# Layer 1's values and gates: a product put ahead, and two row block pairs turned by transposing transfers

## The chip, the cores and the metric

The kernel runs on one core of a Trainium2 chip. The metric is the time of one execution in microseconds (us) on the device, as the median of several runs. TensorE (PE) multiplies matrices, VectorE (DVE) and ScalarE (ACT) do elementwise work, GpSimd (POOL) and SyncE (SP) here mostly issue transfers (DMA). Each engine works through its own row of instructions in order, and waits on semaphores for the others.

## What is computed

A trunk of two layers on 1024 rows of 1024 columns in fp32. Each layer is a token mixer and a squared-ReLU MLP, each with an RMSNorm ahead and a residual add behind; layer 0 mixes by dilated attention, layer 1 by gated linear attention (GLA). The change lies at the start of layer 1's mixer, in the part of its first projection that gives the values v and the output gate:

```python
def gla_mixer(h, w_in, w_gate_up, b_gate, norm_w, w_out):
    proj = h @ w_in
    q, k, v = proj[..., :s1], proj[..., s1:s2], proj[..., s2:s3]
    g_out, gate_lr = proj[..., s3:s4], proj[..., s4:]
    gk = gate_lr @ w_gate_up + b_gate
    log_a = jax.nn.log_sigmoid(gk.astype(jnp.float32)) / GLA_GATE_NORMALIZER
    ...
    gate = jax.nn.silu(g_out.astype(jnp.float32)).reshape(B, S, GLA_HEADS, GLA_DV)
    o = (o * gate).reshape(B, S, GLA_VAL_DIM).astype(h.dtype)
    return o @ w_out
```

## The kernel before

**Precision.** Each fp32 operand is cut into a rounded part (hi, by a copy on ACT) and a remainder (lo, by a subtraction on DVE). A product is three matmuls: hi by hi, hi by lo, lo by hi.

**The seven products.** `Mixed` (L901, on `Values`, L766) multiplies the normed rows, transposed, by 1024 columns twice: group g = 0 is the gate (g_out), g = 1 the values. Both are done in Strassen's manner: the rows' transpose has quarters a11, a12, a21, a22, and the seven products of a group use in this order a12, a11, s1, s2, s4, s3, a22 on the rows' side, where s1 = a21 + a22, s2 = s1 - a11, s4 = a12 - s2, s3 = a11 - a21. On the columns' side stand a block of weights or a sum of blocks (`total`, L803), cut into dh (`rounded`, L825, ACT) and dl (`remain`, L833, DVE). Each product has two steps of 24 + 24 matmuls of 128x512; steps 0 to 13 are group 0 and 14 to 27 group 1. `load` (L781) fetches a step's weights, by SP, some steps ahead.

**Accumulators.** The products go in turn to four banks of PSUM called B (pB) and A (pA): "BABABAB", where a new start clears the bank for a12, a11, s1 and a22, and s2, s4 and s3 accumulate on what is there. `sums` (L873) takes results out: c11 is copied from B (a12's product) and added to what A holds after a11, c22, c12 and c21 likewise. For group 0 the results are tiles gq and gp, which then go through the gate's function: `begin` (exp, ACT), `guard` (DVE), `logs` (two ACT operations), `close` (three DVE operations on gd, ge and the result, and a store to ggscr by SP). c21 of a group is added at the start of the next group's first step (L876).

**Buffers.** Tiles come from pools: 25 buffers `k4` of 128 x 1024 fp32 (weights, dh, dl, gp and others), 12 of `h8`, 8 of `t2`.

**Rows and their transposes.** `Halves` (L308) norms the rows and transposes them. The 1024 rows are four row block pairs p of 256 rows. Pairs p = 0 and 1 are turned by transfers: `send` (L332) copies the 32-bit values on ACT into pieces (`half`) in which the two 16-bit halves lie apart, and POOL stores them to a scratch in HBM (`wscr`); `flip` (L341) reads them back with two transposing transfers on SP's queue. Pairs p = 2 and 3, "pairs 3 and 4", are turned on TensorE: `turn` (L347) issues 16 PE transposes of 128x128 (L355) into banks pT, which ACT copies out (L357).

**Order.** All engines' rows are written out by hand, without a scheduler. `Down.run` and `run_end` (L2008, L2122) finish layer 0's MLP; `hook` (L2029) and `between` (L2063) put the norm, the first cuts and the first loads beside its last steps; `gla_values` (L2171) then issues the 28 steps. Behind them stand the low-rank gate's product (L2462, pd), its result lg (L2466, L2467) and the first gate product (L2364, pg).

Of the kernel before, what the change touches and what calls it, by code (L numbers as in the profile page):

```python
# [9 lines left out]
F32 = mybir.dt.float32  # L10
# [3 lines left out]
U16 = mybir.dt.uint16  # L14
AF = mybir.ActivationFunctionType
# [5 lines left out]
P = 128  # L21
D = 1024
# [20 lines left out]
def hybrid_trunk(ctx, tc, x, norm_mix, norm_mlp, norm_fin, a_in, a_out, g_in, g_up, g_b, g_nw,  # L43
                 g_out, m_up, m_down, tab, msk, gmask, ident_d, out):
    nc = tc.nc
    pe, act, dve, pool, sp = nc.tensor, nc.scalar, nc.vector, nc.gpsimd, nc.sync
# [4 lines left out]
    drp = ctx.enter_context(tc.tile_pool(name="drp", bufs=1, space=DRAM))  # L51
# [5 lines left out]
    def k4(shape, dt, name):  # L57
        return wk.tile(shape, dt, name=name, tag="k4", bufs=25)

    def t2(shape, dt, name):  # L60
        return wk.tile(shape, dt, name=name, tag="t2", bufs=8)
# [241 lines left out]
        for j in range(n):  # L303
            yield tuple(s[j][:, :, sl] if len(s) == n else s[0][:, 2 * j:2 * j + 2, sl] for s in sets)

    wscr = [drp.tile([4 * P * D], U16, name=f"wscr{p}") for p in range(2)]

    class Halves:  # L308

# [19 lines left out]
                for k in range(2):  # L329
                    self.a[p // 2, k] = self.one("a", F32)  # L330

        def send(self, p):  # L332

            for i, t in enumerate(self.xn[p]):
                for k in range(2):
                    part = t2([P, D], U16, "half")
                    act.activation(part.rearrange("p (h c) -> p h c", h=2),
                                   t[:, 512 * k:512 * k + 512].bitcast(U16).rearrange("p (c h) -> p h c", h=2), AF.Copy)
                    pool.dma_start(wscr[p].rearrange("(k i p r) -> k i p r", k=2, i=2, p=P)[k, i], part)
# [181 lines left out]
    class Up:  # L521
# [82 lines left out]
        def product(self, p, s, ks=range(4)):  # L604
            w = self.part[p]
            if s == 6:
                wh, wl = w["d"][:, 0], w["d"][:, 1]
            else:
                wh, wl = (t[:, s % 2] for t in w["aabbgg"[s]])
            h = self.h[self.OPERANDS[s]]  # L610
            st = self.st.setdefault(p, {})
            b = "XYXVXZV"[s]
            first = s in (0, 1, 3, 5)
            if first and ks[0] == 0:
                st[b] = bank("p" + b)
            for k in ks:
                xh, xl = h.parts(k)
                for n, (u, v) in enumerate(((wh, xh), (wh, xl), (wl, xh))):
                    pe.matmul(st[b], u[:, k, :], v, start=first and k + n == 0, stop=k == 3 and n == 2,  # L619
                              skip_group_check=True)  # L620
# [145 lines left out]
    class Values:  # L766
# [3 lines left out]
        ahead = (1,)  # L770
# [24 lines left out]
        def source(self, g):  # L795
            return a_in, g * 3 * AW + 2 * AW
# [36 lines left out]
        def remain(self, n):  # L833
# [2 lines left out]
            dve.tensor_tensor(lo, t, hi.bitcast(F32), op=OP.subtract)  # L836
            self.cut[n] = hi, lo

        def product(self, n, blocks=range(4)):
            g, q, m = self.place(n)  # L840
            s = "BABABAB"[q]
            fresh = q in (0, 1, 2, 6)
            if fresh and m == 0 and blocks[0] == 0:
                self.acc[s] = [bank("p" + s) for _ in range(4)]
            th, tl = self.cut[n]
            for k in range(2):
                sh, sl = self.h[ORDER[q]].parts(2 * m + k)
                for t in blocks:
                    c = slice(128 * t, 128 * t + 128)
                    for v, (a, b) in enumerate(((sh, th), (sh, tl), (sl, th))):  # L850
                        pe.matmul(self.acc[s][t], a[:, c], b[:, k, :], start=fresh and m + k + v == 0,  # L851
                                  stop=m == 1 and k == 1 and v == 2, skip_group_check=True)
# [48 lines left out]
    class Mixed(Values):  # L901

        STEPS = 28
        small = True
        ahead = ()

        def __init__(self):
            super().__init__()
# [1 line left out]

        def source(self, g):
            return g_in, (2048, 1024)[g]

        def copy(self, name, s, t, g):
            if g:
# [499 lines left out]
    hs = Halves(x0, wbc, vals, None)  # L1415
# [330 lines left out]
    plan = [n for n in range(8, vals.STEPS) if n // 14 not in vals.ahead or n % 14 > 1]  # L1746
# [52 lines left out]
    for p in range(heads.count):  # L1799
        h, g = divmod(p, NG)  # L1800
        if g == 1 and h:
            plan_merges(h - 1, 14 * p)
        if p == heads.count - 1:
            for k in range(0, KT, 2):
                add_rows(a_out, k)
            c = 14 * p
# [104 lines left out]
    class Down:  # L1911
# [117 lines left out]
        def hook(self, n):  # L2029
            if n == 40:  # L2030
                self.wbc = load_norm_w(self.next_norm)
            if self.spill is not None:
                if n == 46:
                    self.mixed = Mixed()
                    self.hs = Halves(self.xs, self.wbc, self.mixed, self.spill)
                    self.hs.norm(0)
                elif n == 47:
                    self.hs.send(0)
                elif n == 49:
                    self.hs.norm(1)  # L2040
                    self.hs.flip(0)
                elif n == 50:
                    self.hs.send(1)
                elif n >= 52:
                    if n == 52:
                        self.hs.flip(1)
                    for k in range(2):
                        self.mixed.load(2 * (n - 52) + k)
            elif 44 <= n < 48:
                tb = n - 44  # L2050
                o = k4([P, D], F32, "fin")
                y = row_rstd([self.rows(tb)])
                dve.scalar_tensor_tensor(o, self.rows(tb), y[:, 0:1], self.wbc, op0=OP.mult, op1=OP.mult)
                sp.dma_start(out[0, 128 * tb:128 * tb + 128, :], o)
            elif n >= 52:
                for t in (2 * (n - 52), 2 * (n - 52) + 1):
                    ss, o = self.fin[t] = sm([P, 8], "ss"), k4([P, D], F32, "fin")
                    self.square(t, 512, 512, 1)
                    self.weigh(t, 512, 512)
                    dve.tensor_scalar(ss[:, 3:4], ss[:, 1:2], 1.0 / D, EPS, op0=OP.mult, op1=OP.add)  # L2060
                    dve.tensor_scalar(ss[:, 4:5], ss[:, 3:4], -0.5, None, op0=OP.mult)

        def between(self, t):  # L2063

            hs, mixed = self.hs, self.mixed
            if t == 0:
                mixed.rounded(0)
                hs.cut("a12", 0)
                mixed.remain(0)
            elif t == 1:  # L2070
                hs.rstd(2)
                hs.cut("a12", 1)
                mixed.prep(1)
            elif t == 2:
                hs.norm(2)
                hs.cut("a11", 0)
            else:
                hs.rstd(3)
                hs.cut("a11", 1)
                hs.norm(3)  # L2080
                mixed.prep(2)

        def square(self, t, c, n, k):
            ss, _ = self.fin[t]
# [86 lines left out]
    def gla_values():  # L2171

        hs, m = down.hs, down.mixed
        m.product(0)
        hs.turn(2)
        m.prep(3)
        m.load(4)
        m.product(1, [0, 1])
        m.product(1, [2, 3])
        hs.turn(3)  # L2180
        m.load(5)
        hs.sum1(0)
        m.total(4)
        hs.sum1(1)
        hs.cut("s1", 0)
        m.sums(2)
        m.product(2)
        m.rounded(4)
        m.total(5)
        m.remain(4)  # L2190
        hs.cut("s1", 1)
        m.load(6)
        m.sums(3)
        m.product(3)
        m.rounded(5)
        hs.sum2(0)
        m.remain(5)
        hs.sum2(1)
        hs.cut("s2", 0)
        m.load(7)  # L2200
        m.total(6)
        for n in range(4, m.STEPS):
            if n != 13:
                m.guard()
                m.close()
            if n not in (5, 25):
                m.sums(n)
            if n == 4:
                m.sums(5)
                hs.cut("s2", 1)  # L2210
            if n == 24:
                m.sums(25)
            m.prep(n + 2)
            m.load(n + (4 if n < 5 else 5))
            if n == 4:
                m.load(9)
            m.product(n)
            if n == 4:
                hs.sum4()
                hs.cut("s4", 0)  # L2220
            elif n == 5:
                hs.cut("s4", 1)
                hs.sum3()
                hs.cut("s3", 0)
            elif n == 6:
                hs.cut("s3", 1)
                hs.cut("a22", 0)
            elif n == 7:
                hs.cut("a22", 1)
            if n != 13:  # L2230
                m.logs()
                if n >= 7:
                    m.begin()
            if n + 3 < m.STEPS:
                m.total(n + 3)
            if n == 22:
                plan_gla()
                W.limit = 3
            if n == 23:
                W.dma()  # L2240
                W.dma()
            if n in (20, 21):
                hs.cut("a21", n - 20)
            if n >= 25:
                W.pump()
        for t in range(4):
            m.add("c21", "B", t, 1)
        return [[m.h["a11"], m.h["a12"]], [m.h["a21"], m.h["a22"]]]
# [279 lines left out]
```

## Time and profile before

| | |
|---|---|
| Median of 3 runs | 2573.11 us (2571.94 to 2574.34) |
| Profiled execution: its time, its span | 2571.72 us, 2569.9 us |
| Mean granted TensorE clock | 0.999 |
| PE, DVE, ACT busy | 2557.1, 1863.5, 1316.5 us |
| The changed stretch, first product to first pd | 1555.8 to 1712.5 us |

A row of the timeline reads: start and duration in us, engine, line of the kernel, operation, tile written <- tiles read, shape, count; in brackets how long the engine was idle before it and what it waited for. A count over 1 stands for several instructions of a kind in a row, and the duration is then that of all. Matmuls overlap: they last 0.39 us and start every 0.23 us.

### The profile page before, as it was taken

Reading aid. Unit: us, or ns where it says so; the run is one execution under the profiler, and the core shown is the slowest. Engines: PE = TensorE matmul, PEld = TensorE weight load, DVE = VectorE, ACT = ScalarE, POOL = GpSimd, SP = SyncE. Lnnn points to the kernel's source line nnn. Section 1 sums busy time; section 2 is a strip of 40 time slices with the busy share of each in tenths; the row PEclk is TensorE's granted clock in tenths of the full one; section 3 lists DMA queues with packets and bytes.
Section 4 is the critical chain, followed back from the end, with each engine's and each line's share of the span. In section 5 each row is a group of like instructions: output and inputs, shape, how many; then the busy total and the mean of one; then the engine's idle time right before and its main releaser. Section 6 shows DMA issues by size and latency. Waiting matters only on the chain.

```text
span 2569.9 us, 33110 instructions
## 1 busy us (share of the span) xinstructions
PE 2557.1 (100%) x11888; PEld 2131.6 (83%) x11888; DVE 1863.5 (73%) x3018; ACT 1316.5 (51%) x2371; POOL 62.8 (2%) x99
## 2 busy tenths in 40 slices
PE   9999999999999999999999999999999999999998
PEld 7888888888888888888888888888888888888887
DVE  7745888889888778666657588887658866666667
ACT  7423455656666356555533355655436555453344
POOL 0000000000000000000000000000000000000000
PEclk9999999999999999999999999999999999999999
DMA  5543578787887644544865473462724454495543
GB/s 184 172 137 121 144 185 205 187 203 190 200 209 183 227 148 160 164 148 147 292 246 187 139 237 127 134 197 103 201 89 141 164 168 139 145 350 204 188 141 130
DMA packets 403654, 452.10 MB, mean 176 GB/s; under 512 B 93617, under 2 KB 265521, under 8 KB 403490
## 3 DMA queue, kind: packets, MB, share of 16 engines
q1 hardware_dynamic: 397522, 431.84, 55.1%
q0 software_dynamic: 5824, 17.90, 2.0%
q8 instruction: 93, 1.52, 0.3%
q14 instruction: 71, 0.58, 0.1%
q10 hardware_dynamic: 144, 0.26, 0.0%
HBM read 276.04 MB, written 130.81 MB: 158 GB/s over the span
## 4 chain that ended last, share of the span: by engine, by line
PE 64%; DVE 2%; ACT 1%; issue 0%; DMA 0%; SPq 0%; DVEq 0%; ACTq 0%
PE pB L1984 13%; PE pX L619 10%; PE pA L1984 10%; PE pV L619 7%; PE pY L619 3%; PE pZ L619 3%; PE pd L216 3%; PE pd L214 3%; PE pd L215 3%; PE pB L851 3%; PE pA L851 2%; PE pO L2288 1%; PE pU L2270 0%; PE pO L2287 0%; PE pT L355 0%; DVE dl L836 0%
## 5 line engine op out<-in xcount | busy, mean ns | idle before, releaser
L1984 PE MATMUL pB<-dh 128*128 128x512 f32 x512 | 199.2, 389 | 0.0
L1984 PE MATMUL pB<-dl,dh 128*128 128x512 f32 x512 | 199.2, 389 | 0.0
L1984 PE MATMUL pB<-dh,dl 128*128 128x512 f32 x512 | 199.2, 389 | 0.0
L223 DVE TENSOR_TENSOR dl<-sin,dh 128x1024 fp32r<-128x1024 f32 x112 | 136.6, 1220 | 45.5 <-ACT dh L220 44.9
L220 ACT ACTIVATE dh<-sin 128x1024 fp32r<-128x1024 f32 x112 | 117.8, 1052 | 86.9 <-PE pB L1984 35.8
L220 ACT ACTIVATE dh<-kept 128x1024 fp32r<-128x1024 f32 x64 | 67.9, 1061 | 183.5 <-DVE kept L1949 138.1
L619 PE MATMUL pV<-s4h,wd 128*128 128x512 f32 x448 | 150.9, 398 | 0.0
L1984 PE MATMUL pA<-dh 128*128 128x512 f32 x384 | 149.4, 389 | 0.0
L1984 PE MATMUL pA<-dl,dh 128*128 128x512 f32 x384 | 149.4, 389 | 0.0
L1984 PE MATMUL pA<-dh,dl 128*128 128x512 f32 x384 | 149.4, 389 | 0.0
L1026 ACT ACTIVATE pt<-pt,orow 128x128 f32<-128x128 f32 (+1 forms) x192 | 84.5, 442 | 66.2 <-DVE orow L1024 65.6
L1984 PEld LDWEIGHTS pB<-dl,dh 128*128 128x128 f32 x512 | 96.1, 188 | 20.0
L1984 PEld LDWEIGHTS pB<-dh 128*128 128x128 f32 x512 | 96.1, 188 | 20.0
L1984 PEld LDWEIGHTS pB<-dh,dl 128*128 128x128 f32 x512 | 96.1, 188 | 19.9
L557 DVE TENSOR_TENSOR wal<-raw,wah 128x512 fp32r<-128x512 f32 x112 | 76.2, 686 | 38.5 <-ACT wah L556 38.5
L628 ACT ACTIVATE c<-c 128x512 f32<-128x512 f32 x64 | 40.4, 631 | 118.6 <-DVE c L656 77.5
L557 DVE TENSOR_TENSOR wbl<-t,wbh 128x1024 fp32r<-128x1024 f32 x56 | 68.6, 1225 | 44.2 <-ACT wbh L556 44.0
L619 PEld LDWEIGHTS pV<-s4h,wd 128*128 128x128 f32 x448 | 84.2, 188 | 17.8 <-DVE rb L644 0.4
L223 DVE TENSOR_TENSOR dl<-kept,dh 128x1024 fp32r<-128x1024 f32 x64 | 78.4, 1225 | 24.4 <-ACT dh L220 18.4
L619 PE MATMUL pZ<-a22h,wgh 128*128 128x512 f32 x224 | 89.9, 401 | 0.0
L624 ACT ACTIVATE e<-pX 128x512 f32<-128x512 f32 x96 | 56.5, 588 | 63.9 <-PE pX L619 63.8
L619 PE MATMUL pX<-s3h,wgh 128*128 128x512 f32 x224 | 88.6, 395 | 0.0
(404 smaller groups left out, 7409.9 us busy)
## 6 DMA issues: line engine op xcount, KB each, us to landing
sin<-acts SPq DMA_DIRECT2D x112, 512.0 KB, 3.8
raw<-in_mlp_w_up_dram SPq DMA_DIRECT2D x64, 512.0 KB, 6.1
acts<-s SPq DMA_DIRECT2D x64, 512.0 KB, 3.4
raw<-in_mlp_w_down_dram SPq DMA_DIRECT2D x64, 512.0 KB, 4.8
raw<-in_attn_w_in_dram SPq DMA_DIRECT2D x98, 256.0 KB, 4.8
cw<-c SPq DMA_DIRECT2D x192, 128.0 KB, 2.8
acts<-c SPq DMA_DIRECT2D x64, 256.0 KB, 2.2
kept<-in_mlp_w_down_dram SPq DMA_DIRECT2D x32, 512.0 KB, 5.0
```

Source lines behind the costliest of these rows:

```text
L214: pe.matmul(ps, sh, mh, start=start, stop=False)
L215: pe.matmul(ps, sh, ml, start=False, stop=False)
L216: pe.matmul(ps, sl, mh, start=False, stop=stop)
L220: act.activation(hi, src, AF.Copy)
L223: dve.tensor_tensor(lo, src, hi.bitcast(F32), op=OP.subtract)
L557: self.remain(lambda: dve.tensor_tensor(lo, src, hi.bitcast(F32), op=OP.subtract))
L619: pe.matmul(st[b], u[:, k, :], v, start=first and k + n == 0, stop=k == 3 and n == 2, skip_group_check=True)
L624: act.activation(e, self.st[p]["X"], AF.Copy)
L628: act.activation(r, r, AF.Relu)
L851: pe.matmul(self.acc[s][t], a[:, c], b[:, k, :], start=fresh and m + k + v == 0, stop=m == 1 and k == 1 and v == 2, skip_group_check=True)
L1026: act.activation(pt[:, i, :128 * n], pt[:, i, :128 * n], AF.Exp, scale=-1.0, bias=m, accum_out=self.row[:, r, HD:HD + 1])
L1984: pe.matmul(self.acc[s][t], a[:, k, c], b[:, k, :], start=fresh and m + k + v == 0, stop=m == 7 and k == 1 and v == 2, skip_group_check=True)
```

## The change

Group 1's first product (a12, steps 14 and 15) is computed right after group 0's first, by which a list `PLAN` gives the order of the steps: 0, 1, 14, 15, 2 to 13, 16 to 27. It is accumulated in bank A, which is otherwise first used for group 0's a11, and is copied by ACT (`keep`) into two k4 tiles `c11`, which stay until group 1's a11 is there and are then added as before. c11 of group 0 is copied from bank B right after step 1, four copies in a row, rather than in two pairs. c21 of group 0 is added at step 16 rather than 14, and the gate's function of it comes two steps later too; loads, cuts and totals follow the new order. Pairs p = 2 and 3 are turned by `send` and `flip` rather than `turn`: 8 copies on ACT, 8 stores by POOL and 4 transposing transfers on SP's queue, into the scratch `wscr` that now has four parts, in place of 32 PE transposes and 8 copies from PSUM. `send` may now do one half (k) at a time, and the second a11 cut moves from `between` to `gla_values`, behind the sends.

```diff
@@ Halves.send
-        def send(self, p):
-
-            for i, t in enumerate(self.xn[p]):
-                for k in range(2):
+        def send(self, p, ks=(0, 1)):
+
+            for k in ks:
+                for i, t in enumerate(self.xn[p]):
                     part = t2([P, D], U16, "half")
@@ Mixed
-        ahead = ()
+        ahead = (1,)
+        PLAN = (0, 1, 14, 15, *range(2, 14), *range(16, 28))
+        def side(self, g, q):
+            return "A" if q == 0 and g in self.ahead else super().side(g, q)
+
+        def keep(self):
+
+            for t in range(4):
+                if t % 2 == 0:
+                    pair = k4([P, 2, 512], F32, "c11")
+                c = self.kept["c11", t] = pair[:, t % 2, :]
+                act.activation(c, self.acc["A"][t], AF.Copy)
@@ Down.between
                 mixed.prep(1)
+                hs.cut("a11", 0)
             elif t == 2:
                 hs.norm(2)
-                hs.cut("a11", 0)
+                mixed.load(2)
+                mixed.rounded(14)
             else:
+                hs.send(2, (0,))
                 hs.rstd(3)
-                hs.cut("a11", 1)
+                mixed.remain(14)
                 hs.norm(3)
-                mixed.prep(2)
+                mixed.load(3)
@@ gla_values
         m.product(0)
-        hs.turn(2)
+        hs.send(2, (1,))
+        hs.send(3, (0,))
+        m.prep(15)
+        hs.send(3, (1,))
+        m.load(4)
+        hs.flip(2)
+        m.product(1)
+        for t in range(4):
+            m.copy("c11", "B", t, 0)
+        hs.cut("a11", 1)
+        m.prep(2)
+        m.product(14)
+        m.load(5)
+        hs.flip(3)
         m.prep(3)
-        m.load(4)
-        m.product(1, [0, 1])
-        m.product(1, [2, 3])
-        hs.turn(3)
-        m.load(5)
+        m.total(4)
+        m.product(15)
+        m.keep()
+        m.rounded(4)
+        m.remain(4)
+        m.total(5)
         hs.sum1(0)
-        m.total(4)
...
-        for n in range(4, m.STEPS):
+        plan = (*Mixed.PLAN[6:], *range(m.STEPS, m.STEPS + 6))
+        for i, n in enumerate(Mixed.PLAN[6:]):
+            soon = lambda k: plan[i + k]
             if n != 13:
                 m.guard()
                 m.close()
+            if n == 16:
+                for t in range(4):
+                    m.add("c21", "B", t, 0)
+                    m.c["c11", t] = m.kept.pop(("c11", t))
...
-            m.prep(n + 2)
-            m.load(n + (4 if n < 5 else 5))
+            m.prep(soon(2))
+            m.load(soon(4 if n < 5 else 5))
...
-            if n + 3 < m.STEPS:
-                m.total(n + 3)
+            if soon(3) < m.STEPS:
+                m.total(soon(3))
```

More of the change, by code (lines that the diff above doesn't have):

```diff
@@ L304, in pieces @@
             yield tuple(s[j][:, :, sl] if len(s) == n else s[0][:, 2 * j:2 * j + 2, sl] for s in sets)
-    wscr = [drp.tile([4 * P * D], U16, name=f"wscr{p}") for p in range(2)]
+    wscr = [drp.tile([4 * P * D], U16, name=f"wscr{p}") for p in range(4)]
     class Halves:
@@ L837, in remain @@
             self.cut[n] = hi, lo
+        def side(self, g, q):
+            return "BABABAB"[q]
         def product(self, n, blocks=range(4)):
             g, q, m = self.place(n)
-            s = "BABABAB"[q]
+            s = self.side(g, q)
             fresh = q in (0, 1, 2, 6)
@@ L912, in source, with side @@
             return g_in, (2048, 1024)[g]
+        def side(self, g, q):
+            return "A" if q == 0 and g in self.ahead else super().side(g, q)
[5 more added lines that the diff above has]
+                act.activation(c, self.acc["A"][t], AF.Copy)
         def copy(self, name, s, t, g):
@@ L2047, in hook @@
                     for k in range(2):
-                        self.mixed.load(2 * (n - 52) + k)
+                        self.mixed.load(Mixed.PLAN[2 * (n - 52) + k])
             elif 44 <= n < 48:
@@ L2174, in gla_values @@
         m.product(0)
-        hs.turn(2)
-        m.prep(3)
-        m.load(4)
-        m.product(1, [0, 1])
-        m.product(1, [2, 3])
-        hs.turn(3)
-        m.load(5)
+        hs.send(2, (1,))
[12 more added lines that the diff above has]
+        hs.flip(3)
+        m.prep(3)
+        m.total(4)
[4 more added lines that the diff above has]
+        m.total(5)
         hs.sum1(0)
-        m.total(4)
+        hs.cut("s1", 0)
+        m.product(2)
+        m.load(6)
+        m.rounded(5)
         hs.sum1(1)
[L2185 to L2190, printed above, removed]
         hs.cut("s1", 1)
-        m.load(6)
-        m.sums(3)
+        m.remain(5)
+        m.load(7)
         m.product(3)
-        m.rounded(5)
         hs.sum2(0)
-        m.remain(5)
         hs.sum2(1)
         hs.cut("s2", 0)
-        m.load(7)
         m.total(6)
-        for n in range(4, m.STEPS):
+        plan = (*Mixed.PLAN[6:], *range(m.STEPS, m.STEPS + 6))
+        for i, n in enumerate(Mixed.PLAN[6:]):
+            soon = lambda k: plan[i + k]
             if n != 13:
```

## The prediction

> **What bounds the kernel now.** I read the page first (span, engines, the chain that ended last), then the chain of waits around the end of layer 0, then what the products of line L851 waited for.
>
> ```profile
> span 2569.9 us, 33110 instructions
> ...
> PE 2557.1 (100%) x11888; PEld 2131.6 (83%) x11888; DVE 1863.5 (73%) x3018; ACT 1316.5 (51%) x2371; POOL 62.8 (2%) x99
> ...
> PE 64%; DVE 2%; ACT 1%; issue 0%; DMA 0%; SPq 0%; DVEq 0%; ACTq 0%
> ```
>
> PE is never idle for long: whatever is taken off PE is gained only if PE isn't made to wait elsewhere. The chain of waits inside the changed stretch tells where that is close (start, duration):
>
> ```profile
> 1602.14 1.24 DVE dl L836
> 1603.42 11.06 PE pB L851 x47
> ```
>
> Up to 1603.4 us the chain runs through DVE and ACT, and from there through PE alone. So in the first third of the stretch DVE is the pacemaker with almost no spare. The waits of the products (us, times) say the same; they sum to 1.2 us, near the most that could still be gained beside the turns:
>
> ```profile
>   DVE dl L836: 0.6, 1
>   DVE gq L866: 0.4, 1
>   ACT gq L925: 0.2, 1
> ```
>
> **Removed: the two turns.** PE's timeline around them:
>
> ```profile
> 1555.82 0.39 PE L851 MATMUL pB<-dh,a12h 128*128 128x512 f32 x1
> ...
> 1561.26 1.91 PE L355 MATMUL pT<-ident,xn 128*128 128x128 f32 x16
> 1562.93 0.47 PE L851 MATMUL pB<-dh,a12h 128*128 128x512 f32 x1
> ...
> 1568.50 1.91 PE L355 MATMUL pT<-ident,xn 128*128 128x128 f32 x16
> 1570.16 0.48 PE L851 MATMUL pA<-dh,a11h 128*128 128x512 f32 x1
> ```
>
> The 24 products of a step take 1561.26 - 1555.82 = 5.44 us, so two steps 10.88. From the first product to a11's first is 1570.16 - 1555.82 = 14.34, so the turns cost 14.34 - 10.88 = **-3.46 us** when they go. That is the whole gain on offer.
>
> **Moved: ACT and DVE in the first stretch.** On ACT, between the two a11h copies and the first s1h: before, the second a11h has only statistics in front of it, and the turns' copies (L357) stand behind it.
>
> ```order
> L365 ACTIVATE a11h<-a 128x4x256
> L830 ACTIVATE dh<-kept 128x1024
> L357 ACTIVATE a<-pT 128x2x256 x4
> L830 ACTIVATE dh<-kept 128x1024
> L357 ACTIVATE a<-pT 128x2x256 x4
> L365 ACTIVATE s1h<-s_13457 128x2x256
> ```
>
> After, from the end of the statistics (y) to the same place, with `half` the pieces that are sent out and c the kept c11:
>
> ```order
> L232 ACTIVATE y<-t 128x2
> L337 ACTIVATE half<-xn 128x1024 x4
> L830 ACTIVATE dh<-raw 128x1024
> L337 ACTIVATE half<-xn 128x1024 x2
> L940 ACTIVATE gq<-pB 128x512 x4
> L365 ACTIVATE a11h<-a 128x4x256
> L830 ACTIVATE dh<-kept 128x1024 x2
> L927 ACTIVATE c_13509<-pA 128x512 x2
> L927 ACTIVATE c_13512<-pA 128x512 x2
> L830 ACTIVATE dh<-kept 128x1024
> L365 ACTIVATE s1h<-s_13520 128x2x256
> ```
>
> Six halves, a dh and four gq copies have moved in front of the second a11h, for whose remainder a11l DVE waits, with everything else of DVE queued behind that. Durations:
>
> ```profile
> 1563.37 1.04 ACT L365 ACTIVATE a11h<-a 128x1024 fp32r<-128x1024 f32 x1
> 1564.32 1.05 ACT L830 ACTIVATE dh<-kept 128x1024 fp32r<-128x1024 f32 x1
> 1565.27 2.04 ACT L357 ACTIVATE a<-pT 128x512 f32<-128x512 f32 x4
> ...
> 1572.37 1.07 ACT L925 ACTIVATE gq<-pB 128x512 f32<-128x512 f32 x2
> ```
>
> ```profile
> L337 ACT ACTIVATE half<-xn x8: 1040/1041/1042, 1503.6 to 1531.3; 128x1024 uint16<-128x1024 uint16 x8
> ```
>
> ```profile
> 1564.45 1.23 DVE L367 TENSOR_TENSOR a11l<-a,a11h 128x1024 fp32r<-128x1024 f32 x1 [0.19 <-ACT a11h L365]
> 1565.59 2.73 DVE L253 SCALAR_TENSOR_TENSOR xn<-xs,y,wbc 128x512 f32<-128x512 f32 x4
> ...
> 1602.14 1.23 DVE L836 TENSOR_TENSOR dl<-raw,dh 128x1024 fp32r<-128x1024 f32 x1 [0.86 <-ACT dh L830]
> ```
>
> Copies of 1024 columns follow each other every 0.95 us (1563.37 to 1564.32). So a11h comes later by 6 x 0.95 (halves) + 0.95 (dh) + 4 x 0.53 (gq) + about 0.9 (the third half waits for the last pair's xn) = 9.7 us: a11h at 1573.1, a11l at 1574.2. From there DVE needs to do the same work up to the remainder dl of s4's first step, except that xn's 2.7 us now run inside its wait (-2.7), that step 4's dl waits for its dh (+1.2), and that s1l stands right behind its sums (two short waits, +0.4): dl is ready 9.7 - 2.7 + 1.2 + 0.4 = 8.6 us later. PE reaches s4 only 10.88 (the products put ahead) - 3.46 = 7.4 us later. So the wait at s4 grows by **+1.2 us**. Bounds: 0 (if DVE makes it up) to 3.
>
> **Added: transfers.** The way of pairs 1 and 2, which are turned so already, gives the prices (L339 the half pieces, L345 the transposes; ns, then us from issue to landing):
>
> ```profile
> L339 POOL DMA_DIRECT2D wscr<-half x8: 540/540/549, 1505.0 to 1532.8; - x8
> ...
> DMA to landing us min/median/max: 2.2/3.2/6.7
> ```
>
> ```profile
> L345 SPq DMA_TRANSPOSE a<-wscr x4: 1885/2580/6428, 1516.3 to 1536.2; - x4
> ...
> DMA to landing us min/median/max: 5.0/5.1/10.0
> ```
>
> ```profile
> 1567.18 0.42 SPq L2167 DMA_DIRECT2D gc<-in_gla_norm_w_dram  x1
> ```
>
> The flips stand on SP's queue behind xscr, the gate constants gc (the last at 1567.18) and one load of weights; the loads of the next steps stand behind them and wait with them. The last half ends at 1573.1 - 4 x 0.53 = 1571.0; landed by 1573.2 to 1577.7, median 1574.2. The last transpose may wait one issue (2.6) and takes 5.1: 1581.9 by the medians, 1587.7 by the ends. DVE asks for it (first s1 sum) after a11l, two dl, a total, the wait of 1.2, a dl and a total: 1574.2 + 6 x 1.14 + 1.2 = 1582.2. So the medians are just in time, the ends 5.5 us late, and lateness goes to PE nearly one for one, since DVE is behind already. I take **+0.3 us**, from the medians.
>
> [...]
>
> **Added: two buffers held.** c11 of the second group now keeps two of the 25 k4 buffers from step 15 to steps 18 and 19, and the two gp tiles of c21 are finished two steps later. In the built program the remainders dl of steps 18, 19 and 20 follow each other at one address; so dl of step 19 may be written only when product 18 has ended, and that of 20 when 19 has. Before, dl of step 19 waited for product 17's end:
>
> ```profile
> 1658.11 1.23 DVE L836 TENSOR_TENSOR dl<-kept,dh 128x1024 fp32r<-128x1024 f32 x1 [5.09 <-PE pA L851]
> ...
> 1662.78 1.28 DVE L866 TENSOR_TENSOR c<-pA,c 128x512 f32<-128x512 f32 x2
> 1663.98 1.22 DVE L836 TENSOR_TENSOR dl<-kept,dh 128x1024 fp32r<-128x1024 f32 x1
> ...
> 1666.25 0.42 DVE L943 TENSOR_SCALAR gd<-gd 128x512 f32<-128x512 f32 x1
> ...
> 1668.64 1.28 DVE L866 TENSOR_TENSOR c<-pA,c 128x512 f32<-128x512 f32 x2
> ```
>
> ```profile
> 1663.51 0.39 PE L851 MATMUL pB<-dh,s1h 128*128 128x512 f32 x1
> ...
> 1668.95 0.39 PE L851 MATMUL pA<-dh,s2h 128*128 128x512 f32 x1
> ```
>
> A dl that starts when the product before ends takes 1.23, and PE can do one matmul (0.23) without it: PE waits 1.0 us, at step 19 and again at step 20. And step 20 accumulates on bank A, which holds the sums that c11 is added from: its third block needs DVE's second pair of c11 adds first. These end their first 1668.64 + 0.68 - (1663.98 + 1.22) = 4.1 us after dl of step 20. PE gets through two blocks (six matmuls, five still to go when dl is there) in 1.1 us and waits **3.0** more. Together **+5.0 us**. Bounds: 0 (if the address were free in time) to 6.
>
> **Moved: the gate logarithms.** c21 of the first group is added two steps later, so two closes (gd, ge, gp) and a guard move into DVE's last steps. Before, from the second remainder of W's weights:
>
> ```order
> L153 TENSOR_TENSOR wlo<-raw,whi 128x1024
> L866 TENSOR_TENSOR c_14265<-pA,c_14265 128x512 x2
> L153 TENSOR_TENSOR wlo<-raw,whi 128x1024
> L866 TENSOR_TENSOR c_14310<-pA,c_14310 128x512 x2
> L866 TENSOR_TENSOR c_14533<-pB,c_14533 128x512
> ```
>
> After, the same stretch:
>
> ```order
> L153 TENSOR_TENSOR wlo<-raw,whi 128x1024
> L958 TENSOR_SCALAR gd<-gd 128x512
> L971 TENSOR_TENSOR gd<-gd,ge 128x512
> L972 SCALAR_TENSOR_TENSOR ge<-gd,ge 128x512
> L973 SCALAR_TENSOR_TENSOR gp<-gp,ge 128x512
> L869 TENSOR_TENSOR c_14225<-pA,c_14225 128x512 x2
> L153 TENSOR_TENSOR wlo<-raw,whi 128x1024
> L971 TENSOR_TENSOR gd<-gd,ge 128x512
> L972 SCALAR_TENSOR_TENSOR ge<-gd,ge 128x512
> L973 SCALAR_TENSOR_TENSOR gp<-gp,ge 128x512
> L869 TENSOR_TENSOR c_14270<-pA,c_14270 128x512 x2
> ```
>
> Behind them all stands lg, for which PE's first gate product pg waits:
>
> ```profile
> 1701.42 0.68 DVE L956 TENSOR_TENSOR gd<-gd,ge 128x512 f32<-128x512 f32 x1
> ...
> 1703.47 1.22 DVE L836 TENSOR_TENSOR dl<-raw,dh 128x1024 fp32r<-128x1024 f32 x1
> ...
> 1709.33 1.23 DVE L153 TENSOR_TENSOR wlo<-raw,whi 128x1024 fp32r<-128x1024 f32 x1 [0.27 <-ACT whi L152]
> ...
> 1717.00 0.69 DVE L2467 TENSOR_TENSOR lg<-pd,lg 32x512 fp32r<-32x512 f32 x1 [2.15 <-ACT lg L2466]
> ```
>
> A close takes 1703.47 - 1701.42 = 2.05, two 4.1, the guard 0.4: 4.5 us. The waits that can swallow them are 2.15 and 0.27: **+2.0 us** for pg. Bounds: 0 to 4.5.
>
> **The sum.** -3.46 + 1.2 + 0.3 + 5.0 + 2.0 = +5.0 us. On the profiled execution's 2571.72 us that is 2576.8; its time lies 1.39 below the median of the runs (2573.11), so 2578.2.
>
> **The rivals.**
> - *The covers hold (not slower).* If dl of steps 19 and 20 finds a free buffer, the +5.0 goes, c11's adds come in time and DVE enters the last steps earlier; -3.46 + 1.2 + 0.3 + up to 2.0 gives 2571 to 2573. For it: DVE idles 5.09 us there before. Against: that wait was for a buffer already, and now two fewer are free. Chance 0.17. Even with every wait gone the floor is 2573.1 - 3.5 - 1.2 = 2568.4.
> - *The transposes come late (slower).* If the last lands 2 to 5.5 us after DVE's 1582.2, it decides the stretch: 2580 to 2583.5, and some more where a late load joins. For it: the slack is 0.3 us by medians, and one of four transposes held the queue 6.4 us. Against: the three others took 1.9 to 2.6. Chance 0.22. [...]
> - *Small covers fail at the start.* Product 14 starts at 1555.82 + 10.88 = 1566.7 and its dl, which DVE writes ahead of the last xn (1565.59 before), is ready about 1 us earlier; product 2 follows at 1577.6, when its dl, third in DVE's row after a11l (1574.2 + 3 x 1.14), has just ended. If both come a microsecond later: +2, 2580. Chance 0.08.
>
> **How the numbers follow.** The forecast has 0.53, and lies between 2575 and 2581 by its bounds. A measurement here tells 0.2% (5.1 us) from no change: 2568.0 to 2578.3. The forecast stands at that edge, so it gives half to each side; the first rival nearly all to "same", the others to "slower". Faster 0.05 (only more than the whole gain on offer would do), same 0.42, slower 0.53. The range reaches from the first rival's lower end to the late transposes with a little over: 2571 to 2586.
>
> **What would show it.** In the profile after: no L355 between 1560 and 1571, a11's products straight after step 15's; L836 of step 19 and 20 idle before it with PE as releaser, and PE waiting 1.0, 1.0 and 3.0 us there; a wait of some 2 us of PE for lg before pg; DVE's first s1 sum not released by a transpose. I am wrong if PE shows no wait in steps 18 to 21, or if the s1 sum is released by DMA.

## The result, and the profile after

The changed kernel takes 2590.45 us (median of 6 runs, 2585.88 to 2591.66) against 2572.53 us for the kernel before beside it: a ratio of 1.0064, with a 95% interval of 1.0053 to 1.0075. It is slower, as forecast, but by some 18 us rather than 5, and outside the range. Its profiled execution took 2587.45 us, 15.73 more than the profiled 2571.72 before. Of all timed runs here and below, two that the device ran in a slow state are left out: one of e3 (5845.75 us) and one of the kernel before (12540.62 us). The page after:

```profile
span 2585.5 us, 33072 instructions
...
PE 2560.5 (99%) x11856; PEld 2129.1 (82%) x11856; DVE 1863.8 (72%) x3018; ACT 1319.4 (51%) x2371; POOL 67.5 (3%) x107
...
PE 61%; DVE 4%; ACT 1%; issue 1%; SPq 1%; DMA 1%; DVEq 0%; ACTq 0%
```

The span grew by 15.6 us, PE's busy time by 3.4, though 32 transposes have left it: some matmuls last longer (0.50 to 0.80 us behind a wait, 0.39 otherwise), which no term of the prediction had. In the chain that ended last, SP's queue (SPq) and DMA now have 1% each, against 0% before. Inside the changed stretch (start, duration):

```profile
1563.44 6.53 DMA gc<-in_gmask_dram
...
1571.09 5.15 SPq L345
...
1576.35 5.52 SPq L345
...
1582.60 3.81 SPq L345
...
1586.51 4.34 DMA a<-wscr
```

What the chain runs through here is no longer the work of DVE and ACT, but a line of transfers: a constant, then the four transposes (L345) one behind the other. The waits of the products (now line L854) were 0.6, 0.4 and 0.2 us before; now they are (us, times; the view counts the weight loads' waits as well as the matmuls', so a wait can stand in it twice):

```profile
  DVE dl L836: 10.7, 10
  ACT s1h L365: 6.8, 3
  DVE c L869: 5.8, 2
  ACT dh L830: 1.6, 3
```

Where PE waits for long (the wait stands in brackets):

```profile
1556.68 0.39 PE L854 MATMUL pB<-dh,a12h 128*128 128x512 f32 x1
...
1592.28 0.50 PE L854 MATMUL pB<-dh,s1h 128*128 128x512 f32 x1 [2.80 <-ACT s1h L365]
...
1594.16 0.63 PE L854 MATMUL pB<-dh,s1l 128*128 128x512 f32 x1
...
1620.74 0.50 PE L854 MATMUL pB<-dl,s4h 128*128 128x512 f32 x1 [0.77 <-DVE dl L836]
...
1671.43 0.50 PE L854 MATMUL pB<-dl,s1h 128*128 128x512 f32 x1 [0.94 <-DVE dl L836]
...
1678.11 0.50 PE L854 MATMUL pA<-dl,s2h 128*128 128x512 f32 x1 [0.93 <-DVE dl L836]
...
1682.24 0.80 PE L854 MATMUL pA<-dh,s2h 128*128 128x512 f32 x1 [2.70 <-DVE c L869]
...
1733.64 0.49 PE L2396 MATMUL pg<-lg 96*128 96x512 f32 x1 [1.85 <-DVE lg L2499]
```

To price each place I count PE's rows. From the first product to the first pd stand 672 matmuls, one every 0.2267 us (5.44/24): 152.3 us of work. What a product takes beyond its share is its loss, waits and slowed matmuls together; a wait at a product's first matmul is put to the product before it. The stretch was 156.65 us and is 169.40 (1556.68 to 1726.08). The losses, in us:

| place | predicted | measured |
|---|---|---|
| turns gone | -3.46 | -3.56 |
| group 0: a11, s1, s2 (transfers) | +0.3 | 2.96 + 2.24 + 3.20 = +8.40 |
| group 0: s4 (DVE and ACT late) | +1.2 | 1.26 - 0.54 = +0.72 |
| group 1: s1, s2 (two buffers held) | +5.0 | 1.25 + 5.77 = +7.02 |
| behind the first pd: pg waits for lg | +2.0 | +2.12 |
| a22, and the first product's own start | 0 | 0.17 + 0.86 |
| sum | +5.0 | +15.7 |

The turns saved 0.10 us more than forecast, since the first matmul behind the second one was slow before (0.32 us to the next start, 0.23 otherwise). Four of the five steps came about at their place. The big error is the transfers; the smaller one is that matmuls are slow behind a long wait (one every 0.43 us behind the 2.70 us at s2, against 0.23). The timed runs' median is 3 us above this one profiled run, and no trace shows why.

### The profile page after: what moved, and what is told of

It is laid out like the page before. It is cut to its first block, busy times and chain, and to the rows that moved or that the text cites. A ratio compares the mean times of both kernels' runs of the same rounds, so it can differ in the third digit from the quotient of the medians.

```text
span 2585.5 us, 33072 instructions
## 1 busy us (share of the span) xinstructions
PE 2560.5 (99%) x11856; PEld 2129.1 (82%) x11856; DVE 1863.8 (72%) x3018; ACT 1319.4 (51%) x2371; POOL 67.5 (3%) x107
## 4 chain that ended last, share of the span: by engine, by line
PE 61%; DVE 4%; ACT 1%; issue 1%; SPq 1%; DMA 1%; DVEq 0%; ACTq 0%
PE pB L1999 13%; PE pX L619 10%; PE pA L1999 10%; PE pV L619 7%; PE pY L619 3%; PE pZ L619 3%; PE pd L216 3%; PE pd L214 3%; PE pd L215 3%; PE pB L854 1%; DVE dl L836 1%; PE pA L854 1%; SPq L345 1%; PE pO L2320 1%; PE pU L2302 0%
```

## The experiments

The theory after the result: the four transposing transfers are slow because they run while the 16 DMA engines are full; they and the loads queued behind them hold up DVE, and DVE PE; the held buffers cost the rest. The rivals: the half pieces on ACT and DVE cost by themselves; the transfers only start too late (behind the constants gc); the closes moved to the end decide. All ratios are against runs of the kernel before on the same chip (medians 2573.1 to 2573.4 there).

| kernel | median, us (range) | ratio (95%) | first product to first pd |
|---|---|---|---|
| before | 2572.53 | 1 | 156.65 |
| after | 2590.45 (2585.88 to 2591.66) | 1.0064 (1.0053 to 1.0075) | 169.40 |
| e1 turns on PE | 2584.09 (2581.61 to 2584.99) | 1.0041 (1.0025 to 1.0057) | 164.41 |
| e2 constants later | 2586.97 (2586.12 to 2589.37) | 1.0055 (1.0040 to 1.0071) | 167.61 |
| e3 loads later | 2585.43 (2582.48 to 2586.84) | 1.0046 (1.0029 to 1.0063) | 162.19 |
| e4 = e1 + e3 | 2576.84 (2575.07 to 2578.32) | 1.0014 (1.0005 to 1.0024) | 157.59 |
| e5 plain transfers | 2584.59 (2584.11 to 2586.35) | 1.0046 (1.0030 to 1.0063) | 164.27 |
| e6 less traffic | 2587.13 (2585.73 to 2588.68) | 1.0054 (1.0039 to 1.0069) | 162.83 |
| e7 e4, logarithms at 10, 12 | 2577.61 (2575.64 to 2579.72) | 1.0018 (1.0008 to 1.0027) | 161.71 |
| e8 one pair by transfer | 2579.75 (2577.73 to 2580.18) | 1.0024 (1.0015 to 1.0034) | 163.18 |
| e9 e4, logarithms at 19, 21 | 2578.85 (2577.75 to 2579.25) | 1.0020 (1.0011 to 1.0028) | 162.00 |
| e10 e6 + e3 + e9 | 2582.78 (2581.45 to 2583.27) | 1.0036 (1.0022 to 1.0050) | 161.60 |
| e11 e8, turn put elsewhere | 2576.18 (2575.51 to 2577.36) | 1.0012 (1.0003 to 1.0021) | 160.35 |
| e12 transfers free of traffic | 2578.57 (2576.47 to 2580.09) | 1.0020 (1.0011 to 1.0029) | 156.57 |

All twelve came out slower than they were expected to, by 1 us (e2) to 8 us (e10). Two things that no expectation counted have a part in it: the first product starts 0.5 to 3.2 us later than in the profile of before (more in e6), and in e1, e2, e3, e6 and e12 the matmuls behind pg lose 1.5 to 1.7 us, against 0.1 in after, e4 and e5. The stretch, in the last column, holds neither.

**e1: only the products' order.** Both pairs are turned on TensorE again.

```diff
-                hs.send(2, (0,))
...
-        hs.send(2, (1,))
-        hs.send(3, (0,))
+        hs.turn(2)
         m.prep(15)
-        hs.send(3, (1,))
         m.load(4)
-        hs.flip(2)
...
         m.product(14)
+        hs.turn(3)
         m.load(5)
-        hs.flip(3)
```

> The changed order kept, pairs 3 and 4 turned on TensorE again (16 transposes after product 0, 16 after product 14's predecessor). Theory: of the 18 us, the late transposing transfers carry about 8 to 11, the dl buffers of steps 19 and 20 with the slow clock behind them 7, the gate logarithms in the last steps 2, and the turns saved give -3.5. Then this kernel is before + 7 + 2 + up to 1 = 2581.5 to 2582.5 us, with PE's waits at steps 19 and 20 still there and none over 0.5 us at s1. Rival A, the new order itself makes DVE late at s1 and s2: still some 2590. Rival B, the waits at steps 19 and 20 are a consequence of the late transfers: 2573 to 2575.

The losses at a11, s1 and s2 of group 0 are gone; those of group 1 (1.23 and 5.83) and the wait for lg (1.84) are as in after. PE's rows:

```profile
1616.84 0.50 PE L854 MATMUL pB<-dl,s4h 128*128 128x512 f32 x1 [0.76 <-DVE dl L836]
...
1667.30 0.50 PE L854 MATMUL pB<-dl,s1h 128*128 128x512 f32 x1 [0.93 <-DVE dl L836]
...
1678.09 0.49 PE L854 MATMUL pA<-dh,s2h 128*128 128x512 f32 x1 [2.69 <-DVE c L869]
```

So turning by transfers, with all that it drags along, costs 169.40 - 164.41 + 3.56 = 8.55 us of the stretch for the 3.56 that it saves; the new order by itself makes the stretch 164.41 - 156.65 = 7.76 us longer.

**e2: the constants later.** The nine loads of gc are issued behind the load of step 7, so SP reaches the first transpose sooner.

```diff
-    sp.dma_start(gm, gmask)
...
+    def constants():
+        sp.dma_start(gm, gmask)
...
         m.load(7)
+        constants()
```

> The changed kernel with the nine loads of gate constants issued after load 7 in place of ahead of the flips. Theory: the four transposes are issued one after the other on SP's queue, each holding it 2 to 5.5 us, so what stands ahead of them counts: the first, whose data had landed at 1566 us, starts about 5 us earlier and the first s1 sum comes 4 to 6 us earlier: 2584 to 2586 us. Rival, the transposes take 5 us each because of the stores and loads that run beside them, wherever they start: they only wait elsewhere, 2589 to 2591.

The first transpose starts 4.5 us earlier and little comes of it. The transposes after, and in e2 (ns on the queue, start of the first and last; then us from issue to landing):

```profile
L345 SPq DMA_TRANSPOSE a<-wscr x4: 2032/4479/5520, 1571.1 to 1586.5; - x4
...
DMA to landing us min/median/max: 4.3/7.7/11.3
```

```profile
L345 SPq DMA_TRANSPOSE a<-wscr x4: 2346/5142/6768, 1566.6 to 1585.1; - x4
...
DMA to landing us min/median/max: 4.5/8.3/13.6
```

They hold the queue longer instead, and the last is issued only 1.4 us earlier. The stretch gains 1.8 us. The start of the row is not what limits it; its pace is.

**e3 and e4: the held buffers.** From step 13 on, all loads of weights are issued one step later, so that the remainders of steps 19 and 20 no longer wait for the product just before; e3 is this on the changed kernel, e4 on e1.

```diff
-            m.load(soon(4 if n < 5 else 5))
+            if n != 13:
+                m.load(soon(4 if n < 5 or n > 13 else 5))
```

> The changed kernel with the loads of weights one step later from step 13 on, so that in the built program dl of step 19 takes the buffer of a tile of step 17 and dl of step 20 that of step 18. Theory: the waits of 0.94, 0.93 and 2.70 us there and the slow matmuls behind them go, 7.0 us in the ledger of PE: 2583 to 2584 us. Rival B, these waits come from DVE's lateness and not from the buffers: no change, 2589 to 2591. The loads have 5.4 us less lead, which may cost up to 1 us.

> Both: turns on TensorE and loads one step later. Theory, if the terms add: before + 2 (gate logarithms at the end) + up to 1 = 2574.5 to 2575.5 us. Rival A: 2583. If it comes to 2572.5 or less, the term at the end was not real either.

The three waits of group 1 go: s1 and s2 lose 0.00 and 0.40 in e3, 0 and 0.22 in e4. The stretch gains 169.40 - 162.19 = 7.2 us and 164.41 - 157.59 = 6.8. In e3 only a part of this reaches the time: the wait for lg grows from 1.85 to 2.99 us, and the matmuls behind it lose 1.6 us more than in after.

```profile
1730.02 0.50 PE L2397 MATMUL pg<-lg 96*128 96x512 f32 x1 [2.99 <-DVE lg L2500]
```

e4 is 1.0014 of before: with turns on TensorE and the buffers mended, the new order costs 0.94 us of the stretch (157.59 against 156.65) and the wait for lg.

**e5: the same bytes, not transposed.** The reads of pairs 3 and 4 are plain, and leave the transposing out (the rows then hold other data). As many bytes are written; each read takes a quarter of its part of the scratch, four times.

```diff
-                sp.dma_start(o, wscr[p][512 * 512 * k:512 * 512 * (k + 1)].rearrange("(r c) -> r c", c=512), transpose=True)
+                w = wscr[p][512 * 512 * k:512 * 512 * (k + 1)]
+                if p < 2 or self.spill is None:
+                    sp.dma_start(o, w.rearrange("(r c) -> r c", c=512), transpose=True)
+                else:
+                    w = w.rearrange("(i p h c) -> i p h c", i=2, p=P, h=2)[1, :, 1]
+                    sp.dma_start(o, w[:, None].to_broadcast([P, 4, 512]))
```

> The changed kernel in which the four transposing transfers of pairs 3 and 4 are plain ones of as many bytes written (it leaves the transposing out: the rows' transpose holds other numbers). Theory: transposing is what fills the 16 DMA engines between 1571 and 1591 us; plain ones hold the queue 0.4 us and land in some 5 us, DVE's first s1 sum waits for none of them, and the 8.4 us that the late transposes cost in PE's ledger go: 2581.5 to 2583.5 us. Rival: it is the amount of data and what stands on the queue ahead; then 2587 or more.

The queue is free after 0.4 us, but the data come no sooner than 5.9 us, and DVE still waits for them:

```profile
L350 SPq DMA_DIRECT2D a<-wscr x4: 360/402/522, 1573.0 to 1581.5; - x4
...
DMA to landing us min/median/max: 5.9/8.0/9.9
```

```profile
1587.46 1.29 DVE L376 TENSOR_TENSOR s<-a 128x512 f32<-128x512 f32 x2 [2.27 <-DMA a<-wscr]
```

The stretch gains 169.40 - 164.27 = 5.1 us (the losses at a11 and s1 go, s2's 3.24 stays). The transposing itself is thus worth 5.1 of the 8.55; the rest is left with plain transfers too. The last of them could be issued only at 1581.52, when the last half piece landed, 7.2 us after its own issue: there the amount of traffic costs, without any transposing.

**e6: less traffic.** e2, and the last pair's spilled rows (1 MB) are not written in the last pair's turn; pair 0's are written in their place, early. The output holds other rows there.

```diff
-            if self.spill is not None:
-                sp.dma_start(self.spill[256 * p:256 * p + 256, :].rearrange("(i p) d -> p i d", p=P), self.xs[p])
+            if self.spill is not None and p < 3:
+                for r in (0, 3) if p == 0 else (p,):
+                    sp.dma_start(self.spill[256 * r:256 * r + 256, :].rearrange("(i p) d -> p i d", p=P), self.xs[p])
```

> The constants behind the flips, as in the second run, and also the 1 MB store of pair 4's rows to xscr out of the stretch (its place gets pair 1's rows, some 50 us earlier, so those rows of the result are others). Theory: the transposes are slow because the 16 engines are shared; 1 MB less, some 2.7 us of them at 390 GB/s, brings the last transpose 2 to 3 us forward against the second run: 2584 to 2585.5 us. Rival: the transposes take what they take whatever runs beside: 2586.5 to 2588.

Here the transposes are quicker, and DVE's wait for the last falls from 3.06 to 0.45 us:

```profile
L346 SPq DMA_TRANSPOSE a<-wscr x4: 1792/2414/5212, 1569.0 to 1582.9; - x4
...
DMA to landing us min/median/max: 4.8/5.2/8.7
```

```profile
1587.97 1.29 DVE L372 TENSOR_TENSOR s<-a 128x512 f32<-128x512 f32 x2 [0.45 <-DMA a<-wscr]
```

a11, s1 and s2 lose only 1.18 together, against 1.16 + 1.61 + 3.82 = 6.59 in e2, from which e6 differs by the stores alone. So the same four transposes are nearly on time once 1 MB of stores ahead of them is gone. The time does not show it, since the same helper also spills rows in the layers' output projections, so that the edit moved traffic there too: near 930 to 1050 us, in layer 0, e6 loses 2.2 us, and its first product starts at 1561.01; near 1940 to 2000 us, in layer 1, it loses 1.9 us more. What e6 shows is the stretch, not the time.

**e7, e9: the logarithms earlier.** e4, with two of the gate's results begun at once at steps 10 and 12 (e7) or 19 and 21 (e9), so that the last closes leave DVE's last steps.

```diff
-                    m.begin()
+                    m.begin(2 if n in (10, 12) else 1)
```

> The fourth run (turns on TensorE, loads later) with two gate results begun rather than one in steps 10 and 12, so that the last close comes two steps earlier, as before the change. Theory: PE's wait for lg before pg (1.84 us and slower matmuls, 2.2) goes: 2574 to 2575 us. Rival: the closes only make DVE late somewhere else: 2576 to 2578.

> The fourth run (turns on TensorE, loads later), with the second gate result begun in steps 19 and 21, behind c11's adds, in place of 10 and 12. Theory: the term at the end is DVE's two closes in front of lg; placed where DVE has to wait anyway they cost nothing, and the 2.2 us of pg go without a new wait at c11: 2574 to 2575.5 us. Rival: DVE has no room there either and PE waits in steps 20 to 24: 2576 to 2578.

In both the wait for lg is gone, and neither is faster than e4. PE waits elsewhere instead, in e7 for c11's adds, in e9 in s3 and a22:

```profile
1675.19 0.60 PE L854 MATMUL pA<-dh,s2h 128*128 128x512 f32 x1 [2.12 <-DVE c L869]
```

```profile
1697.40 0.50 PE L854 MATMUL pA<-dh,s3h 128*128 128x512 f32 x1 [1.38 <-ACT c L864]
...
1707.68 0.50 PE L854 MATMUL pB<-dl,a22h 128*128 128x512 f32 x1 [0.91 <-DVE dl L836]
```

The closes are work that has to be done in two steps fewer than before; wherever they are put, DVE or ACT is late behind them.

**e8, e11: one pair by transfer, one on TensorE.** e8 is e7 with pair 3 sent and flipped; e11 is e9 with pair 3 by transfer and pair 4's turn behind product 15. The edit of e11 against e9 is below; that of e8 against e7 is the same without its two lines with `turn(3)`.

```diff
+                hs.send(2, (0,))
...
-        hs.turn(2)
+        hs.send(2, (1,))
...
+        hs.flip(2)
...
-        hs.turn(3)
...
         m.keep()
+        hs.turn(3)
```

> Pair 3 turned by transfers, pair 4 on TensorE, loads later and two gate results early. Two transposes in place of four, started at some 1571 us: the last should land by 1582, when DVE asks. Theory: before - 1.7 (one turn saved) + 0.7 (s4) + up to 1.5 = 2571.5 to 2574 us, hardly to be told from before. Rival: even two transposes land late among the loads: over 2575.

> A version without work left out: pair 3 by transfers, pair 4 turned on TensorE behind product 15, where ACT's copies of it stand behind those of c11 and delay no dh; loads later, gate results as in the ninth run. The eighth run lost 3 us at s2 since ACT waited for the turn before it cut step 3. Theory: that goes; before - 1.7 + 0.7 at s4 + up to 1: 2572 to 2573.5 us, not to be told from before. Rival: the two transposes land too late: 2576 or more.

In e8 DVE's first s1 sum no longer waits. But the copies of pair 4's turn from PSUM wait on ACT for the transposes of pair 3 (5.18 us), though they write other columns of the tile; a dh stands behind them on ACT, and DVE waits for that:

```profile
1576.45 0.60 ACT L357 ACTIVATE a<-pT 128x512 f32<-128x512 f32 x1 [5.18 <-DMA a<-wscr]
```

```profile
1581.49 1.23 DVE L836 TENSOR_TENSOR dl<-kept,dh 128x1024 fp32r<-128x1024 f32 x1 [8.77 <-ACT dh L830]
```

s2 loses 3.06. With the turn behind the kept copies (e11) that loss is gone and one turn is saved (the other costs 1.67), but s4 (0.79), s3 (2.37) and a22 (1.21) of group 1 lose as in e9. At 1.0012 (1.0003 to 1.0021) it stands nearest to before, and is still not below it.

**e10, e12: all the terms together.** e10 joins e6, e3 and e9. e12 takes e6's edit for this norm alone, with e2 and e3. Both write pair 0's rows in place of the last pair's, as e6.

```diff
+            late = self.spill is not None and self.spill is xscr
+            if self.spill is not None and not (late and p == 3):
+                for r in (0, 3) if late and p == 0 else (p,):
```

> The changed kernel's transposes of pairs 3 and 4, with every term taken away that the runs before point to: the constants behind the flips and without pair 4's store to xscr, as in the sixth run (so those rows of the result are others), loads one step later, the gate results as in the run before this. If the terms add: no wait over 1.3 us is left in PE's ledger, first product to first pd 155 us against 156.65 before the change, and no wait of pg: 2571.5 to 2574.5 us. If something that no run has touched is left: 2577 or more.

> The changed kernel, its gate results begun as it does, with the transposes freed as in the sixth run, but in this stretch alone (the sixth and the tenth also moved a store to xmid in the output projections, which cost 2.2 us near 1000 us; here only pair 4's rows in xscr are others), and loads one step later. If the terms add: before's 2573.3 - 3.5 (turns) + 1.3 and 0.7 (DVE behind at s2 and s4, as in the tenth) + 0.4 + 2.2 (lg before pg) = 2574.4; 2573.5 to 2576 us, that is: no gain even with the transposes on time. Rival: the closes, not the transposes, are all that is left, and without the two begun early it beats before: below 2571.5.

e10 loses 2.54, 2.39 and 1.20 us in s4, s3 and a22 of group 1, and 2.2 us in layer 0 and 1.7 in layer 1 as e6 does. e12 has the shortest stretch of all, 156.57 us, without a turn on TensorE. Most of the transfers' lateness is the difference between e3 and e12: 162.19 - 156.57 = 5.6 us. But before had 156.65: what the turns' removal saves is lost again (1.76 in s2, 1.24 in s4, 1.24 in the rest). And the wait for lg is the longest of all, with 1.5 us of slow matmuls behind it, so that the profiled span is 5.1 us longer than before's:

```profile
1606.97 0.50 PE L856 MATMUL pA<-dl,s2h 128*128 128x512 f32 x1 [0.76 <-DVE dl L838]
...
1613.72 0.50 PE L856 MATMUL pB<-dl,s4h 128*128 128x512 f32 x1 [0.76 <-DVE dl L838]
...
1721.67 0.79 PE L2403 MATMUL pg<-lg 96*128 96x512 f32 x1 [3.01 <-DVE lg L2506]
```

## Why the prediction was wrong, step by step

**Turns removed, -3.46: right** (3.56 by the rows). No L355 stands in the stretch, and where they are back (e1), PE loses nothing else in those products.

**The transfers, +0.3: the step that failed.** It was put as "The last transpose may wait one issue (2.6) and takes 5.1: 1581.9 by the medians". The first transpose was issued at 1571.1, but the four held SP's queue 5.15, 5.52, 3.81 and 2.03 us, one behind the other with a load of kept weights between, and the last landed at 1590.85. From the first product that is 34.2 us, where the prediction had 1581.9 - 1555.8 = 26.1:

```profile
1571.09 10.78 SPq L345 DMA_TRANSPOSE a<-wscr  x2
1581.96 0.53 SPq L793 DMA_DIRECT2D kept<-in_gla_w_in_dram  x1
1582.60 5.94 SPq L345 DMA_TRANSPOSE a<-wscr  x2
```

The stores of the half pieces landed late too, up to 9.6 us after their issue (6.7 at most before), but the queue shows no gap in which a transpose waited for them. The durations had been taken from the transposes of pairs 1 and 2, and used as if they belonged to the instruction. These runs show that they go with the traffic beside it: the last transpose lands 34.2 us after the first product in after, 32.3 in e2, and with 1 MB of stores gone 26.8 in e6 and 27.4 in e12. How full the DMA engines were in the same 20 us, before and after (from:to, length, busy time and count of PE, PEld, DVE, ACT, POOL, then PE's granted clock, DMA share, GB/s):

```profile
1571.00:1591.00 20.00, 20.00 (x90) 16.57 (x89) 20.00 (x29) 10.81 (x18) 0.00 (x0) 1.00 0.36 129
```

```profile
1571.00:1591.00 20.00, 18.48 (x82) 14.98 (x80) 7.72 (x8) 9.17 (x14) 1.08 (x2) 1.00 1.10 221
```

In e5 and in e6:

```profile
1573.00:1588.00 15.00, 15.00 (x68) 12.43 (x67) 7.89 (x8) 8.92 (x13) 1.08 (x2) 1.00 1.00 337
```

```profile
1568.00:1588.00 20.00, 20.00 (x90) 16.53 (x90) 12.86 (x18) 15.51 (x23) 3.25 (x6) 1.00 0.97 226
```

Full engines (share 1.10) move 221 GB/s while transposes run, and 337 GB/s with plain transfers (share 1.00); in e6, with less to move, it is 226 GB/s at 0.97. So with transposes in the mix the engines are full at a lower rate, and what runs beside is late (the half pieces' stores took a median of 4.4 us to land, against 3.2 before), the transposes too (7.7 against 5.1). The profile of before had shown it already, and I had not looked there: while pair 1 was flipped, a share of 1.13 went with 180 GB/s, and its first transpose took 6.4 us on the queue.

```profile
1522.00:1526.00 4.00, 4.00 (x19) 3.30 (x19) 3.86 (x8) 0.48 (x1) 0.00 (x0) 1.00 1.13 180
```

The prediction named that the loads behind the flips "wait with them", and gave this no price. DVE's waits in that stretch, of which only the first was foreseen:

```profile
1575.07 1.23 DVE L367 TENSOR_TENSOR a11l<-a,a11h 128x1024 fp32r<-128x1024 f32 x1 [3.56 <-ACT a11h L365]
...
1586.58 1.23 DVE L806 TENSOR_TENSOR kept<-kept 128x1024 f32<-128x1024 f32 x1 [4.52 <-DMA kept<-in_gla_w_in_dram]
...
1590.87 1.29 DVE L371 TENSOR_TENSOR s<-a 128x512 f32<-128x512 f32 x2 [3.06 <-DMA a<-wscr]
```

The load of kept weights that it waited for is the one between the transposes above. That wait costs little by itself: it ends 4.3 us before the last transpose lands, for which the sum would have waited in any case. Together the two waits, 7.6 us, became PE's 2.80 and the waits in s2, and 2.2 us of slow matmuls. The sum reads the columns of pair 3 alone, whose two transposes had landed at 1585.41; yet in after, e2, e5, e6 and e12 it starts within 0.13 us of the landing of pair 4's last transfer. So it waits for all four in the built program, as ACT's copies wait for the transposes in e8; no run tries to part them. The rival "transposes come late" was the case that came about. It had added 2 to 5.5 us to the forecast's other terms, which gave 2580 to 2583.5; the transfers cost 8.4, and the other terms 2.6 us more than forecast. The prediction's own sign for this, a first s1 sum released by a transfer, is the 3.06 above.

**DVE and ACT late at s4, +1.2: there, but not from where it was put.** s4 loses 1.26 after, 0.72 more than before; but e4, without half pieces, loses 1.23 as well. So it comes with the products' order, and that the size is near is luck. What the half pieces cost shows in s2 when the transfers are nearly on time: at most 1.18 (e6) to 1.76 (e12), where DVE still waits 0.45 and 1.05 us for the last transpose. The rival that products 14 and 2 start late did not come about: in after, PE loses nothing at either.

**Two buffers held, +5.0: right in mechanism, too small.** The waits of 1.0, 1.0 and 3.0 us are there as 0.94, 0.93 and 2.70, and a place for the loads that frees the buffers takes all three away (e3, e4). The term is 7.0 because the matmuls behind the 2.70 us run slow:

```profile
1682.20:1693.40 11.20, 11.16 (x42) 9.12 (x43) 6.95 (x10) 6.49 (x10) 0.00 (x0) 0.85 0.26 95
```

PE is busy all these 11.2 us, with 42 matmuls where 49 fit, a loss of some 2 us. The same happens after the 2.80 us at s1:

```profile
1592.20:1597.00 4.80, 4.64 (x12) 2.88 (x12) 4.64 (x7) 2.81 (x5) 0.00 (x0) 0.64 0.83 317
```

Together the slow matmuls behind these two waits are some 4.3 us of the 15.7. No term of the prediction had them.

**The logarithms, +2.0: right** (1.85, 2.12 with the matmuls behind). The wait depends on those ahead of it. In e4 and e12 pg starts 165.2 and 165.4 us after the first product, though PE comes to pd 1.0 us sooner in e12: DVE's row ends no sooner, so pg waits 1.84 us in the one and 3.01 in the other. Before, pg started after 162.2 us and waited for nothing. e7, e9 and e10 take this wait away and find it again in c11's adds, s4, s3 or a22. That is why taking the transfers' and the buffers' losses away (e12) leaves no gain: the gate's work for c21 has two steps less to be done in.

**Still open.** The first product starts 0.5 to 3.2 us later in all the later profiles than in the one of before, apart from layer 0's 2.2 us in e6 and e10; it accrues in the first 800 us, which the change doesn't touch. One profile of before is too little to tell whether that is more than its scatter. It is 0.86 us of the 15.7 here.

## What to carry to other kernels

A transfer's time is to be read from a stretch that is as full as the one it is moved into: look at the DMA share of the target's window first, and price a row of transposing transfers by what each holds the queue there (here a median of 4.48 us at a share of 1.10, where the prediction took 2.6). Work taken off the busiest engine counts only if what replaces it has room on the next ones; here ACT and DVE had none, so even transfers that came nearly in time gave back nothing (a stretch of 156.57 us in e12, 156.65 before). And a product's result that is held longer costs where its buffer is next wanted, which shows in the order of the instructions and can be mended by the order of the loads (here 7.02 us in after, 0.40 in e3).

## What was not expected of the hardware

- PE's granted clock dropped after short waits: in after it is 0.64 in the 4.8 us from the end of the 2.80 us wait on. After the 2.12 us of e7 a matmul starts every 0.43 us rather than 0.227, for some 3.3 us (clock 0.83 from 1675 to 1685 us), and after the 2.12 us of e8 every 0.43 us as well. So waits of 2.12 to 2.80 us were enough. Length alone does not decide: after a wait of 1.84 us before pg, the clock stood at 0.56 in e1 and at 1.00 in e4:

```profile
1729.30:1733.00 3.70, 3.44 (x8) 2.30 (x9) 1.64 (x3) 1.95 (x3) 0.00 (x0) 0.56 1.08 369
```

```profile
1722.90:1726.60 3.70, 3.64 (x16) 2.78 (x17) 1.78 (x4) 2.43 (x4) 0.00 (x0) 1.00 1.08 371
```

- The same transposing transfer held its queue between 1.8 us (e6) and 6.8 us (e2): without the 1 MB of stores beside it the median was 2.41 us (e6), with them 5.14 (e2). In after a store of the half pieces landed after 2.3 to 9.6 us.
